# Bias lines on GpSimd, a quarter of some placed blocks on VectorE, and the keys' product later in VectorE's queue

## The chip, the cores and the metric

The kernel runs on one core of a Trainium2 chip. The metric is the device time of one launch in microseconds (us). The core has four compute engines with a queue each, worked off in order: TensorE (PE in the profile; its weight loads are PEld), VectorE (DVE), ScalarE (ACT) and GpSimd (POOL). SyncE (SP) issues nearly all loads. An instruction that waits for a semaphore holds up everything behind it on its engine.

## The reference

An encoder trunk of two layers on 256 positions of width 2048, float32. Layer 0 mixes tokens with grouped-query attention (mixer A: 16 query heads, 4 key heads, normalised and rotated queries and keys), layer 1 with dilated window attention in three head groups and a shared relative position bias (mixer B). A gated MLP with a width-3 convolution over positions follows each mixer.

```python
for i in range(DEPTH):
    hn = rms_norm(h, mix_norm[i])
    j = i // N_MIXERS
    if i % N_MIXERS == 0:
        h = h + mixer_a(hn, a_w_qkv[j], a_w_o[j], a_q_gain[j], a_k_gain[j])
    else:
        h = h + mixer_b(hn, b_w_qkv[j], b_w_o[j], rel_bias)
    h = h + conv_ffn(rms_norm(h, ffn_norm[i]), w_up[i], conv_w[i], conv_b[i], w_down[i])
return rms_norm(h, final_norm)

# mixer_a
k = axial_rope(rms_norm(k.astype(jnp.float32), k_gain)).astype(h.dtype)
# mixer_b, one head group
bias = rel_bias_g[t5_bucket(rel * dilation)].astype(jnp.float32).transpose(2, 0, 1)
logits = jnp.einsum('bnqchd,bnkchd->bnchqk', qb, kb).astype(jnp.float32) * scale + bias[None, None, None]
```

## The kernel before

**Split products.** Every float32 product is made of three TensorE products of rounded values: a matrix is split into a high part (rounded to fp32r) and a low part (what is left). For weights `split_raw` does it: ACT casts `raw` to `wh` (L128), DVE computes `wl = raw - wh` (L129), for 128x1024 elements at a time. One such split feeds 12 matmuls (L153, L154, L155: two 128-wide token halves m, two slices kt, three products). Split tiles lie in a ring of `NHL` = 3 buffers, so ACT's cast for a split waits until PE has used up the split three before it. Six `raw` buffers take the loads, which SP issues (L145).

**What sets the order.** The program is written in Python generators. `feed` emits the splits and matmuls of a projection and calls `step()` after each half; `step()` advances work that was put off (evacuation, transposes, attention) by one `yield`. A scheduler then orders the instructions of each engine by priority and readiness. Splits are emitted with raised priority (`tc.high_priority(offset=AHEAD)`).

**Placed blocks.** To transpose a 128x1024 tile without TensorE, DVE transposes 32x32 blocks (`turn_blocks`, L335), and `place_blocks` copies the sixteen groups of blocks, each 32 partitions by 256 elements, to where they belong. A string of four letters says who copies the groups of each target quadrant: `p` is GpSimd (L345), `a` ACT (L347), `v` DVE (L349); each letter stands for four copies. `turned` uses `"paaa"`: four copies by GpSimd, twelve by ACT. It is called in two places. `late_transpose` makes the next stage's input `hT` out of the residual `h`, for three of the four column blocks ("chunks") at each of three borders: mixer A to the first MLP, that MLP to mixer B, mixer B to the second MLP. There `tM` is the placed tile, and ACT (L294) and DVE (L297) split it into `xh` parts. `heads_T_dve` turns the keys of mixer A (`k_gen`) and the keys and queries of mixer B (`k_gen`, `s_gen`); L290 and L291 split the placed tile. The up-projections of the MLPs call `place_blocks` with `PLACE = "pava"` (tile `u`).

**The keys of mixer A.** `project2` computes the keys (`a0`) and values (`a1`). When the keys are done, `k_gen` starts: `qk_post` evacuates them (`stg`, L687) and squares them (L797) on ACT, multiplies by the cosines on DVE (L799) and by the sines on GpSimd (L804), adds (L806), sums the squares (L807), and takes the power -1/2 (`rsqrt_mean`: L389 on DVE, L390 on GpSimd). The result `rk` is multiplied into `ro` by DVE (L818). Then three yields, and the keys are turned and split into `kTh` and `kTl`. The values are evacuated and split by `evac_split` (`vh` on ACT, L294; `vl` on DVE, L297).

**The bias lines.** Mixer B needs, for each head, the bias of every relative position as a line in DRAM. `bias_lines` prepares them beside the first MLP: two loads bring a 0/1 matrix `of` and the table `rel_bias` (into `rb`); `oh` is the rounded copy of `of` (ACT, L907); `rs` is the high part of `rb`, with the low part in its upper half (DVE, L908 and L909), and `lh` is `rs` repeated along a free dimension (DVE, L910). Six matmuls (L916) then make the lines.

Of the kernel before, what the change touches and what calls it, by code (L numbers as in the profile page):

```python
# [7 lines left out]
F32 = mybir.dt.float32  # L8
F32R = mybir.dt.float32r
AF = mybir.ActivationFunctionType  # L10
ALU = mybir.AluOpType
AX = mybir.AxisListType

P = 128
# [19 lines left out]
def tile_encoder(ctx: ExitStack, tc: tile.TileContext, x, xT, w_a, w_ao, q_gain, k_gain, w_b, w_bo,  # L34
                 rel_bias, gains, w_up, conv, w_down, final_norm, rope, ident_c, onehot, out):
    nc = tc.nc
# [32 lines left out]
    def ps_tile():  # L69
        bank_at[1] = (bank_at[1] + 1) % 4  # L70
        return bank(4 + bank_at[1], "ps")
# [214 lines left out]
    def split(hi, lo, src):  # L286
        if lo is None:
            copy(hi, src)
            return
        nc.scalar.activation(hi, src, AF.Copy)  # L290
        nc.vector.tensor_tensor(lo, src, hi.bitcast(F32), ALU.subtract)  # L291
# [40 lines left out]
    def turn_blocks(s, pool, tag):  # L332
        t = pool.tile([P, 2, 512], F32, tag=tag, name=nm("tT"))
        for m in range(2):
            nc.vector.transpose(t[:, m], s[:, m])  # L335
        return t

    def place_blocks(o, t, place, part=range(16)):
        tv = t.rearrange("p m (j q c) -> p j m q c", j=4, q=4)
        for i in part:  # L340
            a, b = i // 4, (i // 4 + i) % 4
            dst = o[32 * b:32 * b + 32, :, :, 32 * a:32 * a + 32]
            src = tv[32 * a:32 * a + 32, :, :, b]
            if place[b] == "p":
                nc.gpsimd.tensor_copy(dst, src)  # L345
            elif place[b] == "a":
                nc.scalar.activation(dst, src, AF.Copy)  # L347
            else:
                nc.vector.tensor_copy(dst, src)  # L349

    def turned(o, s, pool, tag):
        t = turn_blocks(s, pool, tag)
        for part in (range(8), range(8, 16)):
            yield
            place_blocks(o.rearrange("p j (m t) -> p j m t", m=2), t, "paaa", part)

    def late_transpose(hT, n, g, pool, tags):
        def put(kt, src):
# [347 lines left out]
            hi, lo = (v[:, 2 * hp:2 * hp + 2, :].rearrange("p a c -> p (a c)") for v in o)  # L706
            split(hi, lo, t)

    def heads_T_dve(o, s, pool, tag):
        hi, lo = o  # L710
        dst = hi if lo is None else s.rearrange("p m c -> p (m c)").rearrange("p (j t) -> p j t", j=4)
        yield from turned(dst, s, pool, tag)
        yield
        if lo is not None:
            split(hi, lo, dst)

    def mixer_a():
        with tc.tile_pool(name="apool", bufs=1) as ap:
# [93 lines left out]
            kT = pair_tile(ap, [P, 4, NT], "kT")  # L812

            def k_gen(accs):
                ro, rk = qk_post(accs, "k")
                for m in range(2):
                    kv = ro[:, m, :].rearrange("p (a c) -> p a c", a=4)
                    nc.vector.tensor_tensor(kv, kv, rk[:, 4 * m:4 * m + 4, None].to_broadcast([P, 4, P]),  # L818
                                            ALU.mult)
                yield  # L820
                yield
                yield
                yield
                yield from heads_T_dve(kT, ro, ap, "sq")

# [66 lines left out]
    def bias_lines(wp, lp):  # L892
        if True:
            of = lp.tile([P, 2, 512], F32, tag="tT", name="of").rearrange("p a c -> p (a c)")
            oh = wp.tile([P, 1024], F32R, tag="wh9", name="oh")
            rb = lp.tile([P, 32], F32, name="rb")[:, :24]
            rs = lp.tile([P, 32], F32R, name="rs")[:, :24]
            nc.gpsimd.memset(rb, 0.0)
            nc.gpsimd.memset(rb[32:33, :], -1e30)
            for i in range(2):  # L900
                nc.gpsimd.dma_start(of[64 * i:64 * i + 64], onehot[:64])
                nc.gpsimd.dma_start(rb[64 * i:64 * i + 32, :], rel_bias)
            yield
            yield
            lh = wp.tile([P, 24, 32], F32R, tag="wl9", name="lh")
            lnt = lp.tile([P, 2, 512], F32, tag="tT", name="lnt")
            nc.scalar.activation(oh, of, AF.Copy)  # L907
            nc.vector.tensor_copy(rs, rb)  # L908
            nc.vector.tensor_tensor(rs[64:], rb[64:], rs[64:].bitcast(F32), ALU.subtract)  # L909
            nc.vector.tensor_copy(lh, rs.bitcast(F32)[:, :, None].to_broadcast([P, 24, 32]))  # L910
            for b in range(6):
                for _ in range(2):
                    yield
                c0, w = ((0, 512), (512, 256), (768, 256))[b // 2]
                t = ps_tile()
                nc.tensor.matmul(t[:, :w], lh[:, 4 * b:4 * b + 4, :].rearrange("p a r -> p (a r)"),  # L916
                                 oh[:, c0:c0 + w], start=True, stop=True)
                ln = lnt[:, b % 2]
                nc.vector.tensor_copy(ln[:, :w], t[:, :w])
                dst = scr0[4 * b:4 * b + 4] if b < 2 else scr1[4 * (b - 2):4 * (b - 2) + 4]  # L920
                for i in range(4):
                    yield
                    nc.gpsimd.dma_start(dst[:, 32 * i:32 * i + 32, :], ln[:, :w])

    def mixer_b(hT, ss_in):
        with tc.tile_pool(name="bpool", bufs=1) as bp:
# [26 lines left out]
            for hf in range(2):  # L953
# [6 lines left out]
                def k_gen(accs, kT):  # L960
                    ks = evac_scaled(bp, accs, rstd)
                    yield
                    yield
                    yield from heads_T_dve(kT, ks, bp, "vl")

                def s_gen(g, accs, kT, bts, nmx=nmx, lsum=lsum, nmv=nmv, probs=probs, e=e):
                    qs = evac_scaled(bp, accs, rstd)
                    qT = pair_tile(bp, [P, 4, NT], "qT", 1, g > 0)
                    yield
                    yield  # L970
                    yield from heads_T_dve(qT, qs, bp, "vl")
                    W = NT if g == 0 else P
                    for i in range(4):
                        yield
                        s = ps_tile()
                        for m in range(2):
                            ks_ = (allp, i) if g == 0 else (allp, i, slice(m * P, (m + 1) * P))
                            mm3(s[:, m * W:(m + 1) * W], qT, kT, (allp, i, slice(m * P, (m + 1) * P)), ks_,
                                True, True)
                        lg = bp.tile([P, 2, NT], F32, tag="lg", name=nm("lg"), bufs=2)  # L980
                        lgv = lg[:, :, :W]
                        b = bts[i] if g == 0 else bts[i][:, None, :].to_broadcast([P, 2, P])
                        nc.vector.scalar_tensor_tensor(lgv, s[:, :2 * W].rearrange("p (m c) -> p m c", m=2),
                                                       SCALE, b, ALU.mult, ALU.add)
                        nc.vector.tensor_reduce(nmv[:, g, :, i], lgv, axis=AX.X, op=ALU.max, negate=True)
                        sl = (2 * g + 1) * 4 + i
                        if g == 0:
                            pr = [hpool.tile([P, NT], F32, tag=f"a{c}{sl}", name=nm("pr")) for c in "hl"]
                        else:
                            pt = hpool.tile([P, NT], F32, tag=f"ah{sl}", name=nm("pr"))  # L990
                            pr = [pt[:, :P], pt[:, P:], pt]
                        for m in range(2):
                            c = 4 * m + i
                            nc.scalar.activation(pr[m], lg[:, m, :W], AF.Exp, bias=nmx[:, g, c:c + 1],
                                                 accum_out=lsum[:, g, c:c + 1])
                        probs.append(pr)
                    if g < 2:
                        return
                    mn = small.tile([P, 8], F32, tag="mn", name=nm("mn"))
                    nc.vector.tensor_tensor(mn, nmx[:, 0, :], nmx[:, 1, :], ALU.min)  # L1000
                    nc.vector.tensor_tensor(mn, mn, nmx[:, 2, :], ALU.min)
                    nc.vector.tensor_tensor(e, mn[:, None, :].to_broadcast([P, 3, 8]), nmx, ALU.subtract)
                    nc.scalar.activation(e, e, AF.Exp)
                    nc.vector.tensor_tensor(lsum, lsum, e, ALU.mult)
                    nc.vector.tensor_tensor(mn, lsum[:, 0, :], lsum[:, 1, :], ALU.add)
                    nc.vector.tensor_tensor(mn, mn, lsum[:, 2, :], ALU.add)
                    nc.vector.reciprocal(mn, mn)
                    nc.vector.tensor_tensor(e, e, mn[:, None, :].to_broadcast([P, 3, 8]), ALU.mult)
# [63 lines left out]
                for g in range(3):  # L1072
                    bts = biases(hf, g)
                    ka = project(w_b, 6 * g + 2 + hf, hT, kgs)
                    kT = pair_tile(bp, [P, 4, NT], "kT", 1, g > 0)
# [94 lines left out]
```

## Time and profile before

| | |
|---|---|
| median of 3 runs | 2253.5 us (2252.55 to 2254.77) |
| the profiled execution, its own time | 2253.57 us |
| its span, first to last instruction | 2251.8 us |
| PE busy | 2235.8 us, 99% |
| DVE busy | 1670.6 us, 74% |
| ACT busy | 1536.3 us, 68% |
| POOL busy | 302.1 us, 13% |
| mean granted TensorE clock | 0.999 |

PE is busy nearly throughout. Mixer A fills about the first 265 us, the first MLP runs to about 980, mixer B to about 1530, the second MLP to the end. In the views quoted below a row is: start (us), duration (us; for several merged instructions, of all), engine, line, operation, output<-input, shapes, count, and in brackets the idle time of the engine ahead of it with what ended that. "L129" is line 129 of the kernel.

### The profile page before, as it was taken

The numbers are of one execution on the slowest core, as the hardware profiler recorded it, in microseconds if no ns is written. First come the engines' busy times: TensorE is split into PE (matmuls) and PEld (weight loads), VectorE is DVE, ScalarE is ACT, GpSimd is POOL, SyncE is SP. The second block draws the span as 40 slices with busy tenths as digits, with TensorE's granted clock in tenths as the row PEclk, the third lists the DMA queues.
The fourth block names the chain that finished last, engine by engine and source line by source line (L and its number), as shares of the span: only waits on it lengthen the run. The fifth ranks groups of instructions, "written<-read, shape, count | busy, mean of one in ns | idle before, by whom it ended". The sixth has DMA issues, their size and how long they took to land.

```text
span 2251.8 us, 28923 instructions
## 1 busy us (share of the span) xinstructions
PE 2235.8 (99%) x10087; PEld 1852.7 (82%) x10087; DVE 1670.6 (74%) x2269; ACT 1536.3 (68%) x2401; POOL 302.1 (13%) x438
## 2 busy tenths in 40 slices
PE   9999999999999999999999999999999999999998
PEld 7788788888888888888888888888888888888886
DVE  6776588888877788866575557565888788688895
ACT  7665777777547777767775777565777755577763
POOL 2211102210001010121130103000101100001101
PEclk9999999999999999999999999999999999999999
DMA  8444656766665655666655565565665656556754
GB/s 303 155 150 150 190 191 212 232 208 193 212 201 187 198 188 185 209 223 204 192 176 185 178 193 168 183 201 184 196 194 192 203 196 209 189 191 192 227 194 136
DMA packets 126500, 437.44 MB, mean 194 GB/s; under 512 B 17313, under 2 KB 18081, under 8 KB 126353
## 3 DMA queue, kind: packets, MB, share of 16 engines
q1 hardware_dynamic: 119744, 425.64, 58.4%
q0 software_dynamic: 6176, 9.39, 1.8%
q8 instruction: 79, 1.29, 0.2%
q14 instruction: 69, 0.56, 0.1%
q10 hardware_dynamic: 432, 0.56, 0.1%
HBM read 429.20 MB, written 6.29 MB: 193 GB/s over the span
## 4 chain that ended last, share of the span: by engine, by line
PE 94%; issue 2%; DVE 1%; ACT 1%; DMA 1%; POOL 1%; SPq 0%; POOLq 0%; DVEq 0%; ACTq 0%
PE acc L154 25%; PE acc L155 25%; PE acc L153 25%; PE acc L278 5%; PE acc L273 5%; PE acc L275 5%; DVE wl L129 1%; PE ps L305 1%; PE ps L309 1%; PE ps L308 1%; PE ps L307 0%; PE ps L868 0%; ACT tM L347 0%; ACT wh L128 0%; DMA xt<-in_xT_dram 0%
## 5 line engine op out<-in xcount | busy, mean ns | idle before, releaser
L129 DVE TENSOR_TENSOR wl<-raw,wh 128x1024 fp32r<-128x1024 f32 x828 | 1018.0, 1237 | 428.5 <-ACT wh L128 426.1
L128 ACT ACTIVATE wh<-raw 128x1024 fp32r<-128x1024 f32 x828 | 872.3, 1058 | 497.1 <-PE acc L155 307.9
L154 PE MATMUL acc<-wl,xh 128*128 128x512 f32 x2176 | 848.0, 390 | 3.8 <-DVE wl L129 3.4
L153 PE MATMUL acc<-wh,xh 128*128 128x512 f32 x2176 | 849.2, 391 | 0.0
L155 PE MATMUL acc<-wh,xh 128*128 128x512 f32 x2176 | 847.6, 390 | 0.0
L154 PEld LDWEIGHTS acc<-wl,xh 128*128 128x128 f32 x2176 | 408.7, 188 | 89.3 <-DVE wl L129 6.1
L155 PEld LDWEIGHTS acc<-wh,xh 128*128 128x128 f32 x2176 | 408.6, 188 | 84.6
L153 PEld LDWEIGHTS acc<-wh,xh 128*128 128x128 f32 x2176 | 409.0, 188 | 83.0
L345 POOL COPY u<-t 32x256 f32<-32x256 f32 x176 | 110.9, 630 | 1013.0 <-DVE t L455 1004.8
L273 PE MATMUL acc<-wh,ah 128*128 128x512 f32 x520 | 202.3, 389 | 0.0
L275 PE MATMUL acc<-wh,al 128*128 128x512 f32 x520 | 202.3, 389 | 0.0
L154 PE MATMUL acc<-wl,ah 128*128 128x512 f32 x480 | 187.0, 390 | 0.5 <-DVE wl L129 0.5
L153 PE MATMUL acc<-wh,ah 128*128 128x512 f32 x480 | 187.2, 390 | 0.1
L155 PE MATMUL acc<-wh,al 128*128 128x512 f32 x480 | 186.8, 390 | 0.0
L347 ACT ACTIVATE u<-t 32x256 f32<-32x256 f32 x352 | 147.7, 420 | 14.0 <-DVE t L455 6.0
L278 PE MATMUL acc<-wl,ah 128*128 128x512 f32 x520 | 145.8, 389 | 0.0
L273 PEld LDWEIGHTS acc<-wh,ah 128*128 128x128 f32 x520 | 97.6, 188 | 20.3
L278 PEld LDWEIGHTS acc<-wl,ah 128*128 128x128 f32 x520 | 97.6, 188 | 20.2
L275 PEld LDWEIGHTS acc<-wh,al 128*128 128x128 f32 x520 | 97.6, 188 | 20.2
L154 PEld LDWEIGHTS acc<-wl,ah 128*128 128x128 f32 x480 | 90.1, 188 | 19.2 <-DVE wl L129 0.9
L153 PEld LDWEIGHTS acc<-wh,ah 128*128 128x128 f32 x480 | 90.1, 188 | 18.9 <-DVE cu L629 0.7
L155 PEld LDWEIGHTS acc<-wh,al 128*128 128x128 f32 x480 | 90.1, 188 | 18.7
(185 smaller groups left out, 1727.9 us busy)
## 6 DMA issues: line engine op xcount, KB each, us to landing
raw<-in_w_up_dram SPq DMA_DIRECT2D x352, 512.0 KB, 4.4
raw<-in_w_down_dram SPq DMA_DIRECT2D x176, 512.0 KB, 4.8
raw<-in_w_b_dram SPq DMA_DIRECT2D x144, 512.0 KB, 4.4
raw<-in_w_bo_dram SPq DMA_DIRECT2D x48, 512.0 KB, 4.3
raw<-in_w_a_dram SPq DMA_DIRECT2D x40, 512.0 KB, 4.8
raw<-in_w_ao_dram SPq DMA_DIRECT2D x32, 512.0 KB, 3.8
raw<-in_w_a_dram SPq DMA_DIRECT2D x16, 256.0 KB, 6.2
h<-in_x_dram SPq DMA_DIRECT2D x4, 512.0 KB, 8.5
```

What stands on the lines that cost most here:

```text
L128: nc.scalar.activation(wh, r, AF.Copy)
L129: nc.vector.tensor_tensor(wl, r, wh.bitcast(F32), ALU.subtract)
L153: nc.tensor.matmul(accs[m], xh, wh[:, j, :], start=st, stop=False)
L154: nc.tensor.matmul(accs[m], xh, wl[:, j, :], start=False, stop=False)
L155: nc.tensor.matmul(accs[m], xl, wh[:, j, :], start=False, stop=sp)
L273: nc.tensor.matmul(acc[k], xh, wh[:, j, :], start=k in fresh, stop=False)
L275: nc.tensor.matmul(acc[k], xl, wh[:, j, :], start=False, stop=False)
L278: nc.tensor.matmul(acc[k], xh, wl[:, j, :], start=False, stop=last[k] == i and j == 1)
L305: nc.tensor.matmul(o, lh[ls], rh[rs], start=start, stop=stop)
L308: nc.tensor.matmul(o, lh[ls], rl[rs], start=False, stop=False)
L345: nc.gpsimd.tensor_copy(dst, src)
L347: nc.scalar.activation(dst, src, AF.Copy)
```

## The change

Three edits.

1. `turned` and `heads_T_dve` take the letters as an argument, with the default `"pava"`: of the sixteen groups of a placed tile GpSimd copies four, ACT eight, DVE four. Mixer B's calls pass `"paaa"` as before. So the keys of mixer A and the three chunks at each of the three borders change.
2. In `k_gen` of mixer A the multiplication by `rk` is emitted three yields later, directly before the last yield.
3. In `bias_lines` the four instructions on `rs`, `lh` and `oh` are GpSimd's.

```diff
-    def turned(o, s, pool, tag):
+    def turned(o, s, pool, tag, place="pava"):
         t = turn_blocks(s, pool, tag)
         for part in (range(8), range(8, 16)):
             yield
-            place_blocks(o.rearrange("p j (m t) -> p j m t", m=2), t, "paaa", part)
+            place_blocks(o.rearrange("p j (m t) -> p j m t", m=2), t, place, part)
...
-    def heads_T_dve(o, s, pool, tag):
+    def heads_T_dve(o, s, pool, tag, place="pava"):
...
-        yield from turned(dst, s, pool, tag)
+        yield from turned(dst, s, pool, tag, place)
...
             def k_gen(accs):
                 ro, rk = qk_post(accs, "k")
+                yield
+                yield
+                yield
                 for m in range(2):
                     kv = ro[:, m, :].rearrange("p (a c) -> p a c", a=4)
                     nc.vector.tensor_tensor(kv, kv, rk[:, 4 * m:4 * m + 4, None].to_broadcast([P, 4, P]),
                                             ALU.mult)
-                yield
-                yield
-                yield
                 yield
                 yield from heads_T_dve(kT, ro, ap, "sq")
...
-            nc.scalar.activation(oh, of, AF.Copy)
-            nc.vector.tensor_copy(rs, rb)
-            nc.vector.tensor_tensor(rs[64:], rb[64:], rs[64:].bitcast(F32), ALU.subtract)
-            nc.vector.tensor_copy(lh, rs.bitcast(F32)[:, :, None].to_broadcast([P, 24, 32]))
+            nc.gpsimd.tensor_copy(rs, rb)
+            nc.gpsimd.tensor_tensor(rs[64:], rb[64:], rs[64:].bitcast(F32), ALU.subtract)
+            nc.gpsimd.tensor_copy(lh, rs.bitcast(F32)[:, :, None].to_broadcast([P, 24, 32]))
+            nc.gpsimd.tensor_copy(oh, of)
...
-                    yield from heads_T_dve(kT, ks, bp, "vl")
+                    yield from heads_T_dve(kT, ks, bp, "vl", "paaa")
...
-                    yield from heads_T_dve(qT, qs, bp, "vl")
+                    yield from heads_T_dve(qT, qs, bp, "vl", "paaa")
```

PE's instructions keep their order. What moves on the other engines is shown at three places; a row with `-` stands there before, one with `+` after the change, one with neither in both.

DVE at the keys of mixer A (`ro` the keys, `rqk` the power, `vl` the values' low parts, `tT` the turned blocks, `wl` the splits):

```order
 L129 TENSOR_TENSOR wl_634<-raw_629,wh_633 128x1024
-L818 TENSOR_TENSOR ro_529<-ro_529,rqk_528 128x512 x2
-L297 SCALAR_TENSOR_TENSOR vl_583<-acc_142,rstd_484,vh_582 128x512
-L297 SCALAR_TENSOR_TENSOR vl_583<-acc_143,rstd_484,vh_582 128x512
+L297 SCALAR_TENSOR_TENSOR vl_581<-acc_142,rstd_484,vh_580 128x512
+L297 SCALAR_TENSOR_TENSOR vl_581<-acc_143,rstd_484,vh_580 128x512
 L129 TENSOR_TENSOR wl_658<-raw_630,wh_657 128x1024
+L821 TENSOR_TENSOR ro_529<-ro_529,rqk_528 128x512 x2
 L335 STREAM_TRANSPOSE tT_626<-ro_529 128x512 x2
 L129 TENSOR_TENSOR wl_686<-raw_681,wh_685 128x1024
+L349 COPY ro_529<-tT_626 32x8x32 x2
 L129 TENSOR_TENSOR wl_704<-raw_682,wh_703 128x1024
```

The product has moved behind the two low parts and one split, and copies of placed blocks stand between the splits (two here, two behind the next split). Further up in the same queue one more split now stands ahead of L799, and L807 ahead of L806; on ACT that split's cast stands ahead of the second `stg`.

ACT at the border of mixer A (`tM` the placed tile, `wh` the splits, `xh` the next input):

```order
 L128 ACTIVATE wh_2328<-raw_2305 128x1024
-L347 ACTIVATE tM_2324<-tT_2325 32x8x32 x6
+L347 ACTIVATE tM_2324<-tT_2325 32x8x32 x4
+L294 ACTIVATE xh_2396<-tM_2324,gain 128x256
 L128 ACTIVATE wh_2356<-raw_2352 128x1024
-L347 ACTIVATE tM_2324<-tT_2325 32x8x32 x6
-L128 ACTIVATE wh_2380<-raw_2353 128x1024
-L294 ACTIVATE xh_2396<-tM_2324,gain 128x256
 L294 ACTIVATE xh_2399<-tM_2324,gain 128x256
 L294 ACTIVATE xh_2430<-tM_2324,gain 128x256
 L294 ACTIVATE xh_2433<-tM_2324,gain 128x256
+L128 ACTIVATE wh_2380<-raw_2353 128x1024
```

Six copies stood ahead of `wh_2356` and six ahead of `wh_2380`, and the four `xh` behind. Now the eight copies stand ahead of `wh_2356` (four of them also ahead of `wh_2328`), and all four `xh` ahead of `wh_2380`.

DVE at the start of the first MLP (`xh` the last input parts):

```order
 L297 SCALAR_TENSOR_TENSOR xh_2687<-ps_2679,gain,xh_2687 128x256
-L908 CAST rs<-rb 128x24
 L129 TENSOR_TENSOR wl_2758<-raw_2738,wh_2757 128x1024
 L297 SCALAR_TENSOR_TENSOR xh_2715<-ps_2710,gain,xh_2715 128x256
-L909 TENSOR_TENSOR rs<-rb,rs 64x24
-L910 CAST lh<-rs 128x768
 L297 SCALAR_TENSOR_TENSOR xh_2718<-ps_2710,gain,xh_2718 128x256
 L129 TENSOR_TENSOR wl_2778<-raw_2773,wh_2777 128x1024
```

The three instructions on `rs` and `lh` are gone from DVE, and the one on `oh` from ACT. On POOL they stand behind the loads and ahead of the first MLP's placed blocks:

```order
 L902 DMA rb<-in_rel_bias_dram 32x24
+L910 CAST oh<-of 128x1024
+L907 CAST rs<-rb 128x24
+L908 TENSOR_TENSOR rs<-rb,rs 64x24
+L909 CAST lh<-rs 128x768
 L345 COPY u_2617<-t_2871 32x8x32 x4
```

The cast of `oh` stands first, though it is written last.

## The prediction

> **What bounds the kernel now.** I read the busy time in stretches of 50 us first, then TensorE's own timeline with the idle time in front of each matmul, then the queues that end those waits.
>
> ```profile
> 50.00:100.00 50.00, 47.53 (x224) 38.57 (x223) 36.76 (x49) 30.88 (x51) 13.60 (x11) 1.00 0.51 169
> 250.00:300.00 50.00, 48.34 (x217) 39.32 (x216) 28.42 (x38) 28.75 (x43) 7.12 (x16) 1.00 0.65 202
> 300.00:350.00 50.00, 50.00 (x223) 41.40 (x222) 43.04 (x69) 42.87 (x70) 6.24 (x11) 1.00 0.58 187
> 1450.00:1500.00 50.00, 50.00 (x222) 41.42 (x221) 30.75 (x36) 35.65 (x60) 4.95 (x8) 1.00 0.62 191
> ```
>
> The first figure after the length is PE, then PEld, DVE, ACT, POOL, granted clock, DMA share and GB/s. From 300 us on PE is as full as in the third and fourth row, at full clock, up to the last 50 us, which the change does not touch; taking work off ACT or DVE is worth nothing there. The change can gain only where PE waits, and that is early: 2.47 us are missing in the second stretch, 1.66 in the sixth. The PE rows with a wait, one with its neighbours:
>
> ```profile
> 54.38 0.50 PE L154 MATMUL acc<-wl,xh 128*128 128x512 f32 x1 [0.17 <-DVE wl L129]
> 59.73 0.39 PE L153 MATMUL acc<-wh,xh 128*128 128x512 f32 x1
> 60.87 0.50 PE L154 MATMUL acc<-wl,xh 128*128 128x512 f32 x1 [0.76 <-DVE wl L129]
> 61.21 0.40 PE L155 MATMUL acc<-wh,xh 128*128 128x512 f32 x1
> 72.97 0.50 PE L154 MATMUL acc<-wl,xh 128*128 128x512 f32 x1 [0.88 <-DVE wl L129]
> 241.19 0.50 PE L154 MATMUL acc<-wl,ah 128*128 128x512 f32 x1 [0.52 <-DVE wl L129]
> 282.15 0.50 PE L154 MATMUL acc<-wl,xh 128*128 128x512 f32 x1 [1.60 <-DVE wl L129]
> ```
>
> Matmuls normally start 0.23 us apart (twelve in 2.72 us, see below). Around 60.87 the steps are 1.14 and 0.34, so that stall costs 0.91 + 0.11 = 1.02 us, which is its listed idle time plus 0.26 (the end of the matmul ahead is drawn over the first 0.15 of it, and the restart is slow by 0.11). I price the others by the same addition: 0.43 at 54.38, 1.14 at 72.97, 0.78 at 241.19, 1.86 at 282.15. PE works without a gap afterwards, so everything behind a stall moves with it and a removed one counts in full.
>
> How much a split of weights normally is ahead is seen here:
>
> ```profile
> 263.08 1.06 ACT L128 ACTIVATE wh<-raw 128x1024 fp32r<-128x1024 f32 x1 [1.66 <-PE acc L155]
> 264.18 1.23 DVE L129 TENSOR_TENSOR wl<-raw,wh 128x1024 fp32r<-128x1024 f32 x1 [1.49 <-ACT wh L128]
> 265.80 1.06 ACT L128 ACTIVATE wh<-raw 128x1024 fp32r<-128x1024 f32 x1 [1.66 <-PE acc L155]
> ```
>
> PE uses up one split in 265.80 - 263.08 = 2.72 us. With three buffers a split starts when PE has two more to work through, 5.44 us, and ends at 265.41, 2.33 us after its start. The lead is some 3.1 us, and any longer delay on ACT or DVE reaches PE.
>
> **The keys' product.** Before, it stood on DVE ahead of the values' low parts and a split, and waited for GpSimd's power:
>
> ```profile
> 54.31 1.22 DVE L129 TENSOR_TENSOR wl<-raw,wh 128x1024 fp32r<-128x1024 f32 x1
> 54.48 2.56 POOL L390 TENSOR_TENSOR rqk<-ms,nhalf 128x8 f32<-128x8 f32 x1 [3.68 <-DVE ms L389]
> 57.07 1.29 DVE L818 TENSOR_TENSOR ro<-ro,rqk 128x512 f32<-128x512 f32 x2 [1.54 <-POOL rqk L390]
> 58.28 1.40 DVE L297 SCALAR_TENSOR_TENSOR vl<-acc,rstd,vh 128x512 fp32r<-128x512 f32 x2
> 59.60 1.21 DVE L129 TENSOR_TENSOR wl<-raw,wh 128x1024 fp32r<-128x1024 f32 x1
> ```
>
> Now the low parts and the split follow at 55.53 and end after 1.40 + 1.21 at about 58.1. PE wants the split at 60.87 - 0.91 = 59.96, so 1.8 us remain and the stall goes: 1.02 us. The power ends at 57.04 and is no longer waited for; the two products run from 58.1 to 59.4. Their transposes, which stood behind the split's end at 59.60 + 1.21 = 60.8, start 1.4 us earlier.
>
> Further up, one split is now issued ahead of the product with the cosines, and on ACT its 1.06 us lie ahead of the second `stg`. So GpSimd's second pair of rotary products starts later, and the chain to the wait at 54.38 is rearranged. Between all of its 0.43 us gained and 1.0 us lost I take nothing: on DVE the sum over the squares moves ahead of the wait for GpSimd's pair, so that it fills time in which DVE stood idle and makes room for the split. The upper loss is that one split's 1.06 us on ACT passed on whole.
>
> **The keys' placed blocks.** ACT's chain to the second stall:
>
> ```profile
> 64.02 2.55 ACT L347 ACTIVATE ro<-tT 32x256 f32<-32x256 f32 x6
> 69.46 1.06 ACT L290 ACTIVATE kTh<-ro 128x1024 fp32r<-128x1024 f32 x1
> 70.56 1.23 DVE L291 TENSOR_TENSOR kTl<-ro,kTh 128x1024 fp32r<-128x1024 f32 x1 [1.64 <-ACT kTh L290]
> 71.70 3.49 DVE L129 TENSOR_TENSOR wl<-raw,wh 128x1024 fp32r<-128x1024 f32 x3
> L349 DVE COPY u<-t 32x256 f32<-32x256 f32 x176 | 64.4, 366 | 5.9
> ```
>
> DVE takes `kTl` in order, waits 1.64 us for `kTh`, and the split behind is late. ACT now places 8 blocks and not 12: 4 x 0.42 (2.55 / 6) = 1.7 us less, and it starts 1.4 us earlier, so `kTh`, `kTl` and the split come about 3.1 us sooner, the split at 68.6, done by 69.8. PE wanted it at 72.97 - 0.88 - 0.15 = 71.94, and now 1.02 sooner, at 70.9. One microsecond is left: 1.14 us gained. DVE's four copies (1.5 us by the last row) fit into the idle time ahead of `kTl`. GpSimd's share of the blocks stays at four. The queries behind, which TensorE transposes, are unchanged.
>
> **The border of mixer A.**
>
> ```profile
> 236.25 2.54 ACT L347 ACTIVATE tM<-tT 32x256 f32<-32x256 f32 x6
> 238.82 1.06 ACT L128 ACTIVATE wh<-raw 128x1024 fp32r<-128x1024 f32 x1
> 239.79 1.69 ACT L294 ACTIVATE xh<-tM,gain 128x256 fp32r<-128x256 f32 x4
> 239.91 1.22 DVE L129 TENSOR_TENSOR wl<-raw,wh 128x1024 fp32r<-128x1024 f32 x1 [2.43 <-ACT wh L128]
> ```
>
> PE wanted this split at 241.19 - 0.52 - 0.15 = 240.52. It came late because ACT placed twelve blocks ahead of `wh`, of which these six are the last. Two chunks follow each other here (the second's transposes wait until the first's copies have read their buffer), and ACT is relieved of 1.7 us in each. Against that, this chunk's four `xh` (1.69 us), which stood behind that `wh`, now stand ahead of it. Net 1.7 us sooner: the split is done at 239.4, a lead of 1.1 us. DVE's four copies use the 2.43 us in which it now waits. Gained: 0.78.
>
> At the other two borders I find no PE wait, so ACT's relief is worth nothing there, and DVE takes 4 x 0.366 = 1.5 us more for each of three chunks. Behind the first MLP it idles ahead of the second chunk's transposes:
>
> ```profile
> 942.27 1.31 DVE L335 STREAM_TRANSPOSE tT<-h 128x512 f32<-128x512 f32 x2 [2.45 <-issue]
> ```
>
> That alone covers one chunk's copies, and the lead of 3.1 us twice as much. Behind mixer B DVE is busy for 30.75 of 50 us (first fence). The price taken is nothing; without any cover 4.4 us would be lost at each border.
>
> **The bias lines.**
>
> ```profile
> 279.54 1.06 ACT L907 ACTIVATE oh<-of 128x1024 fp32r<-128x1024 f32 x1 [3.66 <-DMA of<-in_onehot_dram]
> 280.77 0.18 DVE L908 CAST rs<-rb 128x24 fp32r<-128x24 f32 x1 [5.78 <-DMA rb<-in_rel_bias_dram]
> 280.87 1.23 DVE L129 TENSOR_TENSOR wl<-raw,wh 128x1024 fp32r<-128x1024 f32 x1
> 284.82 0.39 PE L153 MATMUL acc<-wh,xh 128*128 128x512 f32 x1
> 285.27 0.50 PE L154 MATMUL acc<-wl,xh 128*128 128x512 f32 x1
> ```
>
> This is the largest stall, and it is a queue's: a cast of 24 columns waits 5.78 us on DVE for its load, and a split that needs neither stands behind. ACT waits 3.66 us the same way. Both go to GpSimd. The split can run as soon as DVE's earlier work ends, 280.77 - 5.78 = 275.0, several us ahead of its need: 1.86 us gained, and the late follower at 285.27 (0.45 instead of 0.23) gives some 0.3 more: 2.2.
>
> GpSimd's casts have no row. Nearest:
>
> ```profile
> L345 POOL COPY tM<-tT x36: 389/396/2399, 219.3 to 1504.2; 32x256 f32<-32x256 f32 x36
> L804 POOL TENSOR_TENSOR t<-stg,st_q 128x256 f32<-128x256 f32 x16 | 15.8, 1016 | 72.1 <-ACT stg L687 72.1
> 299.30 0.97 POOL L345 COPY u<-t 32x256 f32<-32x256 f32 x2 [25.04 <-DVE t L455]
> ```
>
> Scaled from 256 elements to 1024 + 768, seven times: 2.7 us at the least, 16.8 at the most; I take 7.1 by L804, whose partitions are the same 128. From 280.8 even the worst ends at 297.6, before GpSimd's next block at 299.30, ahead of which it idles for 25 us. So on its own queue the price is nothing; with that cover gone the block, and DVE's work on it, would be late by what the casts exceed 18.5 us. Whether they hold up DVE is weighed below.
>
> **Sum.** 1.02 + 1.14 + 0.78 + 2.16 = 5.1 us. The profiled execution took 2253.57 us in all (span 2251.8), 0.1 from the median: 2253.57 - 5.1 = 2248.5, and 2248.4 against the median.
>
> **Rivals.** *Half of the keys' gain stays away.* The later second `stg` puts GpSimd's pair in the way, the wait at 54.38 grows by up to 1.0 us, and the leads of some 1.1 us worked out for the waits at 72.97 and 241.19 are used up. For it: these leads are thin. Against: they lie behind chains that get shorter by 1.7 us and more, so they vanish only if DVE's four copies, put between its splits, cost it as much as ACT saves. Left are 2.2 (bias) and 1.0 to 1.5 of the rest: 2250.1.
>
> *GpSimd's casts stop DVE: slower.* In the chain of waits, and on DVE:
>
> ```profile
> 46.00 1.13 POOL t L804 x2
> 47.39 3.42 POOL t L804 x2
> 48.45 1.76 DVE L129 TENSOR_TENSOR wl<-raw,wh 128x1024 fp32r<-128x1024 f32 x1
> ```
>
> Alone a GpSimd product takes 0.57 us and a split 1.22; side by side 1.71 and 1.76, as if each waited out the other. The casts are long, so a split could wait for a whole one. Up to 3.1 us the lead swallows it; the excess goes to PE. At L804's rate a cast is 4.1 us: 1.0 lost, 2249.5. At the slowest row, 16.8 - 3.1 = 13.7 lost if the split gets in only behind both: 2262. With the 5.1 us gained elsewhere the result is slower from a hold of 8.2 us on, and by more than 4.5 us from 12.7 us on. Against: DVE's turn can come between two casts, and the 2399 ns row is one of 36 whose median is 396. The Trainium skill (SBUF — State Buffer, "Who interferes with whom") has this as a rule: a VectorE instruction with two SBUF inputs and a GpSimd one that reads SBUF exclude each other for the whole instruction. These rows agree (1.76 - 1.22 = 0.54, one product's 0.57).
>
> *The cover at a later border is thinner than it looks.* Then one or two of DVE's copies reach PE, about 1 us: 2249.5.
>
> **Numbers.** 0.2% (4.5 us) is what a measurement here can tell from no change. The forecast has 0.64 (own range 2247.2 to 2249.8), the keys' rival 0.19, GpSimd's hold 0.09, the later border 0.06, a loss that I see nowhere 0.02. Faster by over 0.2%, under 2249.0: nine tenths of the first and a little of the hold and the border, where they come cheap, 0.60. Slower by over 0.2%: a third of the hold and the unseen loss, 0.05. Within: 0.35. The range reaches down to all listed stalls gone (0.4 more) and the runs' scatter of 1.3, 2246.7, and up to the bias gain alone plus 1.2: 2252.5.
>
> **What would show it.** Right: no PE wait at about 60, 72, 240 and 281 us; GpSimd's casts between 280 and 290; PE at 50.00 in every stretch from 300 us on. Wrong: the 54.38 wait above 1 us; a split longer than 3 us beside a cast; a PE wait for `wl` after 900 us. If the stretch 250 to 300 still lacks more than 1 us of PE, the bias term has failed.

## The result and the profile after

| | before | after |
|---|---|---|
| median, 13 runs of each on one chip | 2253.82 us (2252.55 to 2256.77) | 2249.14 us (2248.30 to 2249.68) |
| the profiled execution, its own time | 2253.57 us | 2249.14 us |

The change takes 4.7 us off: the ratio is 0.9978 with a 95% interval of 0.9970 to 0.9987, that is 0.13 to 0.30% faster, and the interval excludes no change. The forecast was 5.1 us, 2248.4.

The busy time of the engines in stretches, as the prediction read it, now of the kernel after (stretch, its length, PE, PEld, DVE, ACT, POOL, granted clock, DMA share, GB/s):

```profile
50.00:100.00 50.00, 49.36 (x243) 41.22 (x242) 40.39 (x58) 31.08 (x50) 14.30 (x11) 1.00 0.55 179
250.00:300.00 50.00, 50.00 (x227) 41.36 (x226) 30.35 (x37) 27.83 (x40) 9.48 (x19) 1.00 0.68 203
1450.00:1500.00 50.00, 50.00 (x222) 41.42 (x221) 33.66 (x44) 32.39 (x54) 5.50 (x9) 1.00 0.61 191
2150.00:2200.00 50.00, 49.46 (x219) 40.55 (x218) 46.12 (x47) 28.47 (x35) 8.92 (x4) 1.00 0.65 215
```

The second stretch of the program lacked 2.47 us of PE and now lacks 0.64. The sixth lacked 1.66 and is now full. In the third row, where the last border's blocks are placed, DVE has more work (33.66 us, 30.75 before) and PE stays full. From 300 us on, the last stretch aside, two stretches are not full: the one from 900 us lacks 0.22 us of PE (0.15 before), and the one in the last row, full before, lacks 0.54. PE's waits, summed by what they wait for (total us, times, longest), in the view of waits of before and then of after; rows of the program's first microseconds are left out:

```profile
PE acc L154 <- DVE wl L129: 3.9, 5, 1.6
```

```profile
PE acc L153 <- DVE cu L629: 0.8, 2, 0.5
PE ps L309 <- DVE qTl L291: 0.6, 1, 0.6
```

The five waits for a split of weights (`wl`, L129) are gone, the one of 54.38 us among them. Priced as in the prediction (from one start to the next, plus 0.11 us for the restart), the six late matmuls of before, at 54, 61, 73, 241, 282 and 285 us, cost 0.44 + 1.02 + 1.15 + 0.79 + 1.87 + 0.32 = 5.6 us. The wait for the queries (`qTl`) has 0.6 us in both.

So 0.9 us less was won by the medians than the stalls cost in the profiled execution of before, and 1.2 less in the two profiled executions (4.4). Most of the difference lies where no edit reaches. The first 45 us took longer in the profiled execution of after, as the same cast on ACT shows, 43.13 us before and 43.63 after (one fence each):

```profile
43.13 1.06 ACT L128 ACTIVATE wh<-raw 128x1024 fp32r<-128x1024 f32 x1 [1.66 <-PE acc L155]
```

```profile
43.63 1.06 ACT L128 ACTIVATE wh<-raw 128x1024 fp32r<-128x1024 f32 x1 [1.66 <-PE acc L155]
2184.62 0.50 PE L153 MATMUL acc<-wh,ah 128*128 128x512 f32 x1 [0.54 <-DVE cu L629]
```

That is 0.50 us; in the thirteen traces of this case the cast starts between 43.03 and 44.23 us, and all three edits lie behind it. At 2184.62, in the second MLP, PE waits until DVE has read an accumulator; by the same price 0.82 us, where before has no wait. At 922 us a wait of the same kind costs 0.49 (before, at 927, 0.42). 5.6 - 0.5 - 0.8 - 0.1 = 4.2, against the 4.4 measured. Whether these waits belong to the change is asked in the last experiment.

### The profile page after: what moved, and what is told of

It is laid out like the page before. It is cut to its first block, busy times and chain, and to the rows that moved or that the text cites. A ratio compares the mean times of both kernels' runs of the same rounds, so it can differ in the third digit from the quotient of the medians.

```text
span 2247.4 us, 28923 instructions
## 1 busy us (share of the span) xinstructions
PE 2234.9 (99%) x10087; PEld 1853.0 (82%) x10087; DVE 1686.3 (75%) x2306; ACT 1519.2 (68%) x2360; POOL 302.0 (13%) x442
## 4 chain that ended last, share of the span: by engine, by line
PE 98%; DVE 1%; DMA 1%; issue 0%; ACT 0%; POOL 0%; SPq 0%; POOLq 0%; DVEq 0%
PE acc L153 26%; PE acc L154 26%; PE acc L155 26%; PE acc L273 5%; PE acc L275 5%; PE acc L278 5%; PE ps L305 1%; PE ps L309 1%; PE ps L308 1%; DMA xt<-in_xT_dram 1%; PE ps L307 0%; PE ps L868 0%; DVE wl L129 0%; PE ps L381 0%; PE ps L704 0%
## 5 line engine op out<-in xcount | busy, mean ns | idle before, releaser
L129 DVE TENSOR_TENSOR wl<-raw,wh 128x1024 fp32r<-128x1024 f32 x828 | 1018.1, 1236 | 418.1 <-ACT wh L128 415.5
```

The costliest lines, as they stand in the source:

```text
L129: nc.vector.tensor_tensor(wl, r, wh.bitcast(F32), ALU.subtract)
```

## The experiments

All times are medians beside the kernel before on the same chip: 2254.05 us (33 runs) beside the four kernels that make a part of the change alone, 2254.24 (29 runs) beside the four first variants of the changed kernel (without the keys' blocks, `oh` on ACT, the eight casts, the queries' scaling), 2253.87 (19 runs) beside the changed kernel repeated and the two kernels sent with it.

**Each edit alone.** First, the bias lines alone:

```diff
-            nc.scalar.activation(oh, of, AF.Copy)
-            nc.vector.tensor_copy(rs, rb)
...
+            nc.gpsimd.tensor_copy(rs, rb)
...
+            nc.gpsimd.tensor_copy(oh, of)
```

> The kernel before with the bias lines' four instructions on GpSimd and nothing else changed. Theory (three separate queue waits whose prices add): the PE stalls of 1.86 + 0.3 us at 282 and 285 us vanish, the ones at 54, 61, 73 and 241 us stay as they were; 2.2 us faster than before, about 2251.6 us where before is 2253.8. Rival (GpSimd's casts hold up VectorE through the shared port): a wl split beside a cast lasts over 3 us and a PE wait for wl stands at 278 to 290 us; gain under 1.2 us. Rival (the gain in the mixer came from a shift of the whole schedule): no gain, 2253.8.

Measured 2251.88 us, 2.2 less (ratio 0.9990, 0.9981 to 0.9999). In the view of stretches and the view of waits of this kernel:

```profile
250.00:300.00 50.00, 50.00 (x228) 41.34 (x227) 30.34 (x38) 30.11 (x47) 11.13 (x23) 1.00 0.66 212
```

```profile
PE acc L154 <- DVE wl L129: 2.3, 4, 0.9
```

The stretch is full, and of the five waits only the largest, 1.6 us, has gone. This edit is worth what its stall cost in the profile of before.

Second, the keys' product alone, three yields later, with the old letters everywhere:

```diff
                 ro, rk = qk_post(accs, "k")
+                yield
+                yield
+                yield
                 for m in range(2):
...
-                yield
-                yield
-                yield
                 yield
```

> The kernel before with only the keys' product emitted behind the values' low parts. Theory: the stall at 61 us (1.02) vanishes; the keys' high part comes 1.4 us sooner against PE's 1.0 to 1.5, so most of the stall at 73 us (1.14) stays, 0.7 to 1.2 us; the stall at 54 us, which the whole change removed too, vanishes here as well if it hangs on the order of the reduction and the split that the product's move brings (0.43). Gain 1.0 to 1.9 us, about 2252.3. Rival (the blocks, not the product, cured the keys): the stall at 61 us stays, gain under 0.5.

Measured 2251.24 us, 2.8 less (ratio 0.9986, 0.9977 to 0.9995): more than I had expected. All three stalls in the keys are gone, not the one:

```profile
PE acc L154 <- DVE wl L129: 1.8, 2, 1.3
```

What is left of the waits for `wl` is one at 239 us (0.52) and the bias lines' (1.33). The timeline says why. Before, then with the product moved alone:

```profile
67.69 1.23 DVE L129 TENSOR_TENSOR wl<-raw,wh 128x1024 fp32r<-128x1024 f32 x1 [2.35 <-ACT wh L128]
70.56 1.23 DVE L291 TENSOR_TENSOR kTl<-ro,kTh 128x1024 fp32r<-128x1024 f32 x1 [1.64 <-ACT kTh L290]
71.70 3.49 DVE L129 TENSOR_TENSOR wl<-raw,wh 128x1024 fp32r<-128x1024 f32 x3
```

```profile
67.84 1.06 ACT L128 ACTIVATE wh<-raw 128x1024 fp32r<-128x1024 f32 x1
68.81 1.04 ACT L290 ACTIVATE kTh<-ro 128x1024 fp32r<-128x1024 f32 x1
68.94 1.23 DVE L129 TENSOR_TENSOR wl<-raw,wh 128x1024 fp32r<-128x1024 f32 x1 [2.00 <-ACT wh L128]
70.08 1.22 DVE L291 TENSOR_TENSOR kTl<-ro,kTh 128x1024 fp32r<-128x1024 f32 x1
71.22 2.35 DVE L129 TENSOR_TENSOR wl<-raw,wh 128x1024 fp32r<-128x1024 f32 x2
```

`kTh` on ACT starts only 0.65 us sooner (68.81 against 69.46, in an execution whose first 45 us took 0.6 us longer). But with the transposes earlier, the scheduler has put a split's cast ahead of `kTh`, and on DVE that split ahead of `kTl`: three splits stood behind `kTl`, now two do. DVE waits for that cast in the time in which it used to wait for `kTh`, and the split ends at 70.2 instead of 72.9.

Third, the keys' placed blocks alone:

```diff
-            place_blocks(o.rearrange("p j (m t) -> p j m t", m=2), t, "paaa", part)
+            place_blocks(o.rearrange("p j (m t) -> p j m t", m=2), t, place, part)
...
-                yield from heads_T_dve(kT, ro, ap, "sq")
+                yield from heads_T_dve(kT, ro, ap, "sq", "pava")
```

> The kernel before with only the keys' placed blocks shared out as pava (borders as before). Theory: the stalls at 54 and 61 us stay, the keys' high part comes 1.7 us sooner and the stall at 73 us (1.14) vanishes; 1.1 us faster, about 2252.7. Rival (ScalarE's copies do not set the keys' end): the stall at 73 us stays over 0.8 us and the time is that of before.

Measured 2252.93 us, 1.1 less (ratio 0.9993, 0.9985 to 1.0002; the interval includes no change). The trace is clear where the time is not: the stall at 73 us is gone, and those at 54 and 60.77 stand unchanged (0.17 and 0.77 of idle time), as does the border's (0.51). The bias lines' stall, which this edit does not touch, has 0.78 of idle time here and not 1.60; that is taken up with the bias lines.

So the product alone removes the stall at 73, and the blocks alone remove it too. Whether the changed kernel needs both is asked by taking the keys' blocks out of it:

```diff
-                yield from heads_T_dve(kT, ro, ap, "sq")
+                yield from heads_T_dve(kT, ro, ap, "sq", "paaa")
```

> The changed kernel with the keys' placed blocks back to paaa (the borders keep pava). Theory formed after the product alone removed all three of the keys' stalls: the keys' blocks add nothing once the product is later, because the split that stood behind the keys' low part is then ahead of it; no stall at 54, 61 or 73 us, 2249.1. The prediction's account (each of the two removes its own stall): a stall of 0.7 to 1.2 us stays at about 72 us, 2250.2.

Measured 2248.55 us (ratio to before 0.9975, 0.9966 to 0.9984). Its view of waits has no wait for such a split:

```profile
PE ps L309 <- DVE qTl L291: 0.6, 1, 0.6
```

(The two rows left out belong to the first microseconds of the program.) Beside the moved product the keys' blocks win no time. But they change how the stall is avoided. Without them the order on DVE is that of the product alone, one split more ahead of `kTl` (the split at 69.00 us, `kTl` at 70.14). With them, in the changed kernel, DVE's order is that of before, and `kTh` comes early:

```profile
66.10 1.06 ACT L290 ACTIVATE kTh<-ro 128x1024 fp32r<-128x1024 f32 x1
67.19 1.23 DVE L291 TENSOR_TENSOR kTl<-ro,kTh 128x1024 fp32r<-128x1024 f32 x1 [0.36 <-ACT kTh L290]
68.34 2.35 DVE L129 TENSOR_TENSOR wl<-raw,wh 128x1024 fp32r<-128x1024 f32 x2
```

`kTh` starts 3.4 us sooner than before, DVE waits 0.36 us for it instead of 1.64, and the split behind `kTl` starts at 68.34 instead of 71.70. There are two ways past this stall, and either is enough.

**The borders.** The new letters at the three borders, nothing else changed:

```diff
-    def turned(o, s, pool, tag):
+    def turned(o, s, pool, tag, place="pava"):
...
-    def heads_T_dve(o, s, pool, tag):
+    def heads_T_dve(o, s, pool, tag, place="paaa"):
```

> The kernel before with only the three borders' placed blocks as pava. Theory: the stall at 241 us (0.78) vanishes, no new PE wait at the two later borders; 0.8 us faster, about 2253.0. Rival (VectorE's twelve more copies reach PE at a later border): new PE waits for wl at 930 to 980 or 1430 to 1540 us, and 0 to 4 us slower than before. The stall of 0.8 us that the changed kernel shows at 2184 us for the accumulators of the down projection: if it comes from the borders' copies it is here too, if it is scatter or comes from elsewhere it is not.

Measured 2253.68 us, 0.4 less (ratio 0.9995, 0.9986 to 1.0004): too little for the time to tell. The wait at 241 us is gone, those at 55, 62, 74 and 282 remain, and no wait for a split arises behind 900 us. The profiled execution also has a wait for an accumulator at 2189 us, of 0.51 us. The test from the other side was sharper: the changed kernel with the old letters everywhere, beside the changed kernel itself.

```diff
-    def turned(o, s, pool, tag, place="pava"):
+    def turned(o, s, pool, tag, place="paaa"):
...
-    def heads_T_dve(o, s, pool, tag, place="pava"):
+    def heads_T_dve(o, s, pool, tag, place="paaa"):
```

> The changed kernel with the old letters everywhere (four blocks by GpSimd, twelve by ScalarE): only the keys' product and the bias lines are left of the change. Theory (the block copies are worth the wait at the border of mixer A and nothing else): a wait for a split of some 0.5 us idle comes back at about 240 us, none at 54, 61 or 73 us, and the time is 0.6 to 1.0 us above the changed kernel's. Rival (with the other two edits the border is relieved anyway, as the keys were): no wait there, and the same time.

Measured 2249.65 us, 1.05 above the changed kernel in the same batch (2248.60). Its timeline at the border:

```profile
233.67 2.55 ACT L347 ACTIVATE tM<-tT 32x256 f32<-32x256 f32 x6
236.24 1.06 ACT L128 ACTIVATE wh<-raw 128x1024 fp32r<-128x1024 f32 x1
237.33 1.23 DVE L129 TENSOR_TENSOR wl<-raw,wh 128x1024 fp32r<-128x1024 f32 x1 [2.43 <-ACT wh L128]
238.61 0.50 PE L154 MATMUL acc<-wl,ah 128*128 128x512 f32 x1 [0.52 <-DVE wl L129]
```

In the changed kernel the same place reads:

```profile
233.59 1.29 ACT L294 ACTIVATE xh<-tM,gain 128x256 fp32r<-128x256 f32 x3
234.79 2.00 ACT L128 ACTIVATE wh<-raw 128x1024 fp32r<-128x1024 f32 x2
236.05 2.35 DVE L129 TENSOR_TENSOR wl<-raw,wh 128x1024 fp32r<-128x1024 f32 x2
```

With six copies (2.55 us) ahead of the cast the split is late by 0.52 us, as before; without them the split follows its cast and PE does not wait. Unlike in the keys, the blocks are needed here, and this is the only wait for a split that they remove: none came back at 54, 61 or 73 us. The 1.05 us are not the border's alone, though. Its wait costs 0.78 by the price used above, and this trace has three more, at 923, 1852 and 2185 us (0.66, 0.53 and 0.30), of the kind that the last experiment is about.

**The bias lines: which wait, and the casts' price.** In the changed kernel, the cast of `oh` back on ACT and the three on `rs` and `lh` left on GpSimd:

```diff
-            nc.gpsimd.tensor_copy(oh, of)
+            nc.scalar.activation(oh, of, AF.Copy)
```

> The changed kernel with the cast of oh left on ScalarE; rs and lh stay on GpSimd. Theory: the stall at 282 us was VectorE's wait for rel_bias, but ScalarE's wait for the 0/1 matrix alone is late too: its cast waits until 276.5 to 277 us, the next split's high part is ready at about 278.5 and its low part at 280, where PE wants it at about 279.9, so a stall of 0 to 0.8 us remains at 280; about 2249.5. Rival (either wait alone gives the whole stall): 1.5 to 2.2 us slower than the changed kernel, 2251.

Measured 2248.80 us (ratio 0.9977, 0.9968 to 0.9986), no different from the change. ACT and DVE in that trace:

```profile
276.06 1.06 ACT L910 ACTIVATE oh<-of 128x1024 fp32r<-128x1024 f32 x1 [3.54 <-DMA of<-in_onehot_dram]
278.46 3.93 DVE L129 TENSOR_TENSOR wl<-raw,wh 128x1024 fp32r<-128x1024 f32 x3 [0.47 <-ACT wh L128]
279.54 0.39 PE L153 MATMUL acc<-wh,xh 128*128 128x512 f32 x1
280.06 0.50 PE L154 MATMUL acc<-wl,xh 128*128 128x512 f32 x1
```

ACT still waits 3.54 us for `of`, and DVE behind it, but PE's step at 280.06 is 0.52 us instead of 0.23: with the restart 0.4 us. So ACT's wait alone would have cost 0.4 of the 2.2 us. The other half, DVE's three instructions left in place with `oh` on GpSimd, was not run. But four kernels leave the bias lines as they were, and their loads landed at different moments. From the start of a load's last issue to the instruction that waits for it, and the price of the stall at 280 to 282 us (all us):

| | `rb` to `rs` on DVE | `of` to `oh` on ACT | the stall |
|---|---|---|---|
| before | 7.01 | 6.30 | 1.87 |
| the keys' product alone | 6.74 | 5.88 | 1.60 |
| the borders alone | 6.41 | 6.34 | 1.27 |
| the keys' blocks alone | 6.20 | 5.79 | 1.04 |

The last of them reads:

```profile
278.72 0.18 DVE L908 CAST rs<-rb 128x24 fp32r<-128x24 f32 x1 [4.97 <-DMA rb<-in_rel_bias_dram]
280.10 0.50 PE L154 MATMUL acc<-wl,xh 128*128 128x512 f32 x1 [0.78 <-DVE wl L129]
```

The stall is DVE's figure less 5.14 to 5.16 us in all four, and it does not follow ACT's. So DVE's short cast, which waited for `rb`, set it. And it is no fixed price: the profile from which the prediction read it has the largest of the four.

Then the casts' price. The cast of `oh` is made eight times over in the changed kernel:

```diff
-            nc.gpsimd.tensor_copy(oh, of)
+            for _ in range(8):
+                nc.gpsimd.tensor_copy(oh, of)
```

> The changed kernel with the cast of oh made eight times on GpSimd (seven needless, same result), some 11 us of casts from 277 us on. Theory: a VectorE split that meets a cast waits for that one cast, at most 1.2 us, gets its turn before the next, and the lead of 3.1 us swallows it: splits of 1.8 to 2.5 us beside the casts, no PE wait, 2249. Rival of the prediction (casts hold the port back to back): a split waits for several casts, lasts over 4 us, and PE stalls for the excess over 3.1 us; up to 8 us slower, 2250 to 2257.

Measured 2248.64 us (ratio 0.9976, 0.9967 to 0.9986), so the rival falls. First the changed kernel, then this one, from the third cast on:

```profile
275.80 1.23 DVE L129 TENSOR_TENSOR wl<-raw,wh 128x1024 fp32r<-128x1024 f32 x1 [0.58 <-ACT wh L128]
276.71 1.22 POOL L910 CAST oh<-of 128x1024 fp32r<-128x1024 f32 x1 [5.43 <-DMA of<-in_onehot_dram]
277.87 0.20 POOL L907 CAST rs<-rb 128x24 fp32r<-128x24 f32 x1
278.16 0.23 POOL L908 TENSOR_TENSOR rs<-rb,rs 64x24 fp32r<-64x24 f32 x1
278.45 0.83 POOL L909 CAST lh<-rs 128x768 fp32r<-128x768 f32 x1
278.52 1.84 DVE L129 TENSOR_TENSOR wl<-raw,wh 128x1024 fp32r<-128x1024 f32 x1 [1.50 <-ACT wh L128]
294.02 1.89 POOL L345 COPY u<-t 32x256 f32<-32x256 f32 x4 [14.73 <-DVE t L455]
```

```profile
280.34 1.05 POOL L911 CAST oh<-of 128x1024 fp32r<-128x1024 f32 x1
281.32 1.88 POOL L909 CAST lh<-rs 128x768 fp32r<-128x768 f32 x1
283.15 7.22 POOL L911 CAST oh<-of 128x1024 fp32r<-128x1024 f32 x5
286.68 1.68 DVE L129 TENSOR_TENSOR wl<-raw,wh 128x1024 fp32r<-128x1024 f32 x1 [1.41 <-ACT wh L128]
289.40 2.05 DVE L129 TENSOR_TENSOR wl<-raw,wh 128x1024 fp32r<-128x1024 f32 x1 [1.05 <-ACT wh L128]
```

The four instructions take 1.22 + 0.20 + 0.23 + 0.83 = 2.5 us, and GpSimd still idles 14.73 us ahead of its next block. A split beside them takes 1.84 us instead of 1.23. The five splits beside the eight casts take 1.61, 1.23, 1.31, 1.68 and 2.05 us. The largest excess, 0.82, is less than one cast, so each split had its turn after one cast at the most; the five casts in a row took 7.22 us.

**A further version.** The wait that is left, for the queries at 86 us, has the form of two of those removed: DVE's scaling of the power (8 columns) waits for GpSimd, and splits stand behind. It goes to GpSimd, behind the power:

```diff
-                nc.vector.tensor_scalar(rq, rq, SCALE, None, op0=ALU.mult)
+                nc.gpsimd.tensor_scalar(rq, rq, SCALE, None, op0=ALU.mult)
```

> The changed kernel with the queries' scaling of the power (VectorE, 8 columns, in mixer A's attend) moved to GpSimd, where the power itself is computed. Theory (a small instruction that waits on VectorE for another engine stalls the splits queued behind it): VectorE no longer waits 1.5 us for the power ahead of two splits and the queries' low part, and the wait of 0.86 us at 86 us vanishes; 0.9 us faster than the changed kernel, 2248.2. Rival (that wait is set by TensorE's transposes and ScalarE's queries' high part): it stays, and the time is 2249.1.

Measured 2247.74 us (ratio to before 0.9972, 0.9962 to 0.9982); the three variants beside it have 2248.55 to 2248.80. Run again beside the changed kernel itself:

> The changed kernel with the queries' scaling on GpSimd, in the same batch as the changed kernel itself. Theory: TensorE's wait at about 86 us (0.86 us) is gone and the time is 0.7 to 1.1 us below the changed kernel's. Rival: the lower time of the first such run was scatter; the difference is under 0.4 us although the wait is gone.

Measured 2248.05 us (ratio 0.9971, 0.9960 to 0.9983) against 2248.60 for the changed kernel. First the changed kernel, then this second run:

```profile
83.05 0.17 DVE L831 TENSOR_SCALAR rqk<-rqk 128x8 f32<-128x8 f32 x1 [1.53 <-POOL rqk L390]
85.41 1.28 DVE L291 TENSOR_TENSOR qTl<-ps,qTh 128x512 fp32r<-128x512 f32 x2
86.15 0.39 PE L309 MATMUL ps<-kTh,qTl 128*128 128x256 f32 x1 [0.60 <-DVE qTl L291]
```

```profile
82.78 1.05 POOL L831 TENSOR_SCALAR rqk<-rqk 128x8 f32<-128x8 f32 x1
83.65 1.28 DVE L291 TENSOR_TENSOR qTl<-ps,qTh 128x512 fp32r<-128x512 f32 x2
85.06 0.28 PE L309 MATMUL ps<-kTh,qTl 128*128 128x256 f32 x1
```

The wait (0.60 us idle, 0.86 by the prediction's price) is gone in both runs. The time is 0.8 to 1.1 us lower in one batch and 0.55 in the other, below the 0.7 that I had expected at the least and above the rival's 0.4. The second profile again has a wait for an accumulator at 2183 us (0.54), and one for a split at 2181.69 (0.17), which the changed kernel has in neither of its profiles. The median was the lowest in each batch, but single runs overlap with those beside it (2247.07 to 2249.10 against 2248.15 to 2249.20), so how much of the 0.86 arrives is open.

**Do the later waits belong to the change?** The changed kernel once more, unedited:

> The changed kernel a second time, beside the next two. Theory: the small waits around 922 to 927 us and at 2184 us (0.49 and 0.82 us in the first profile of this kernel) come from when loads land and differ again, by some tenths of a microsecond or by their absence; the time stands 4.5 to 5.5 us below before. Rival: they belong to the change, and both come again within 0.1 us of 0.49 and 0.82.

Measured 2248.60 us (ratio 0.9974, 0.9964 to 0.9984), 5.3 us below before where the first measurement has 4.7. Its stretches, beside 49.46 at 2150 us in the first profile:

```profile
900.00:950.00 50.00, 50.00 (x223) 41.31 (x222) 47.55 (x60) 36.25 (x56) 6.67 (x8) 1.00 0.65 212
2150.00:2200.00 50.00, 50.00 (x222) 41.34 (x221) 46.97 (x47) 29.13 (x36) 8.94 (x4) 1.00 0.66 218
```

Both waits are absent from an execution of the very same kernel. A wait at 2183 to 2189 us stands in five of the eight traces with the new letters at the borders (0.3 to 0.8 us) and in two of the five with the old ones (0.3 and 0.6), so no edit decides it. So the 0.9 us that the first median lacks is not tied to an edit. Some of it may be the bias lines' stall, which the profile of before has at its largest. For the later waits, that they come from when loads land is the likeliest reading, since DVE's waits for the loads of the MLPs' second weights differ too, in the view of waits of the first profile and of this one:

```profile
DVE raw L242 <- DMA raw<-in_w_down_dram: 14.3, 12, 3.0
```

```profile
DVE raw L242 <- DMA raw<-in_w_down_dram: 11.7, 10, 2.2
```

No run changed a load to show it, so that stays open.

## Why the prediction was right, and where it was not

- **The bound.** Right in the main: only PE's early waits were won, and behind 300 us no wait for a split was gained or lost by ACT's relief or DVE's copies. But PE was not full from 300 us on in every stretch of before (49.85 from 900 us), and the sign "PE at 50.00 in every stretch" failed in the first profile of after, with 49.78 and 49.46. The second has 50.00 in both.
- **The keys' product, 1.02 us.** The step was right: the split that was to end at about 58.1 us ended at 57.96 (56.75 + 1.21, in a program that by then ran 0.5 us late), and the stall is gone. What this edit is worth was mis-sized, since the same move alone also removes the stalls at 54 and 73: 2.6 us by the trace, 2.8 by the time of that edit alone.
- **The wait at 54.38, taken as nothing.** Mis-sized by the 0.43 us at the good end of the bounds given. What the prediction described, the sum over the squares filling DVE's idle time, is what happened; the loss that stood against it did not.
- **The keys' placed blocks, 1.14 us.** The path was right, the price was not the blocks' own. The prediction let `kTh`, `kTl` and the split come some 3.1 us sooner, the split at 68.6; `kTh` came 3.4 us sooner and the split at 68.34, and DVE's four copies took 1.5 us, as forecast. What failed is the adding of 1.14 to 1.02: it holds only if the stall stays without the blocks, and it does not. Without them the scheduler puts one split more ahead of `kTl`, and the time is the same. I had costed the two edits one after the other and never asked what the first leaves for the second.
- **The border of mixer A, 0.78 us.** Right: gone with the blocks, back without them (0.52 us idle; the 1.05 us of time hold other waits too). At the other borders no wait for a split arose, as forecast.
- **The bias lines, 2.16 us.** Right: 2.2 measured alone. The prediction did not divide it between the two queues; DVE's cast set it. That the number fits so well is in part luck, since the stall was 1.04 to 1.87 us in four executions and the prediction read the one of 1.87.
- **GpSimd's casts.** Mis-sized: 2.5 us against 7.1 taken and a lower bound of 2.7. The 7.1 came from products with two inputs, whose mean of 1.02 us holds waits for DVE; alone one took 0.57. GpSimd's next block began 17.3 us after the first cast (276.71 to 294.02), so the size changed nothing. The casts lay at 277 to 279 us, not between 280 and 290, as the program was ahead there. The hold is there and costs 0.6 us of a lead of some 3.
- **The keys' rival** (half of the gain stays away) fell: the wait at 54 went instead of growing. **The sum** of 5.1 against 4.7 is two errors of opposite sign, 0.4 more won at 54 and some 0.9 that differs from one execution to the next (the start, the bias lines' stall, the late waits). That they nearly cancel is luck.

## What to carry to other kernels

On an engine that works in order, look for short instructions that wait long for another engine or a load: casts and scalings of 0.2 us in VectorE's queue cost TensorE 2 us in one place and 0.9 in another. When two edits may cure the same stall, test each alone and each left out: one may already do what the other was priced for. Price a stall on TensorE from one start to the next with the restart. If a stall hangs on a load, read it in several executions before taking its price, and expect gains under one microsecond to drown in loads that land differently.

## What the runs showed of the hardware

- GpSimd and VectorE hold each other up in both directions: beside the eight casts a split took 1.23 to 2.05 us against 1.23, the cast of `lh` 1.88 instead of 0.83, and five casts in a row 7.22 us where one alone takes 1.05. The excess of a split never exceeded one cast. The Trainium skill (SBUF — State Buffer, "Who interferes with whom") has the exclusion for the whole instruction; that a split gets in between the casts of a row is what these runs add. They have no two splits directly in a row.
- GpSimd's cost of a cast with one input is far below that of its products with two: 1.05 us for 1024 elements in each partition and 0.83 for 768, so 0.22 us for 256 more and 0.86 ns an element, against 0.57 us that a product of 256 took alone. The Trainium skill (GPSIMD Engine Reference, "3.1 Elementwise — side-by-side cycle accounting") states 1.03 cycles an element for the shortest loop bodies and 2.6 for two inputs; at the 1.2 GHz of its example the first is, by estimate, 0.86 ns, and the trace agrees.
- A scaling of 8 columns took 1.05 us on GpSimd with a split beside it, and 0.17 on VectorE; on GpSimd TensorE's wait for it was gone all the same.
